# Hybrid decoder step on one core: the weight split of a mixture-of-experts loop, parts 4 and 5 moved across a branch

## The chip, the cores and the metric

The kernel runs on one core of a Trainium2 chip. The metric is device time in microseconds, the median of several runs. TensorE (PE) multiplies matrices, VectorE (DVE) and ScalarE (ACT) work element by element, GpSimd (POOL) issues gathers and scatters by index, and SyncE (SP) issues the loads. Each engine runs its own instructions in order and waits for others by semaphores.

## The reference

One layer of a decoder for 2048 prompt rows and 32 sample rows, 1024 wide: normalised input projection, dilated window attention beside a state-space mixer, output projection, and then a mixture of 32 experts, of which each row takes two. The change lies in the expert stage only:

```
def expert_block(args):
    xb, e = args
    hid = jax.nn.silu(xb @ w_gate[e]) * (xb @ w_up[e])
    return hid @ w_down[e]
# w_gate, w_up: (32, 1024, 512); w_down: (32, 512, 1024)
# y[token] = sum over its two experts of gate * expert_block(row)
```

All values are 32 bit floats. The kernel keeps their precision on PE by splitting each operand into a rounded part h and a rest l = x - h, and by adding three products, h*h, h*l and l*h.

## The kernel before

The routing stage leaves, for each expert in an order that it chooses (`R.order`), the number of its rows (`R.cnt`) and lists of row numbers in groups of 128. The function `moe` then runs 32 experts p = 0 to 31, unrolled, with instructions in the order of the text. One block (`block`) works on 128 rows of one expert. An expert with up to 128 rows runs only `main(p)`, one block. One with more runs one to three blocks of `further(p, b)` ahead of it, inside the branches at L2130, L2132 and L2134; the branch at L2130 is skipped for the small ones.

The weights of one expert come in six parts of 1 MB: parts 0 to 3 hold gate and up (two of eight slices of the 1024 rows each, 2 x 512 KB), parts 4 and 5 hold down. `E.load(p, i)` (L1906) issues part i of expert p on SP into the buffer `raw` i; there is one buffer for each part. `E.hi` (L1934) lets ACT cast the buffer to `wh`, `E.lo` (L1937) lets DVE subtract to get `wl`. A pair (wh, wl) lies in one of eight places; part i of expert p takes place (6p + i) mod 8, so that parts 2, 3, 4, 5 of the next expert take the places of parts 0, 1, 2, 3 of this one, and must wait until PE has read these. A load into a buffer waits for the subtraction that read it.

A block: PE multiplies slices 0 to 3 for both halves of the hidden width (`up`, L2003), then slices 4 to 7 for half 0, then it transposes the 128 x 1024 rows of the next block into PX (`turned`, L1993), then slices 4 to 6 of half 1; it transposes half 0 of the hidden values (`hidT(0)`, L2011), multiplies slice 7 of half 1, takes a quarter of the down product (L2020), transposes hidden half 1, and takes the other three quarters. Between these stand, on ACT and DVE, the Silu (L2006) and the product with up (L2007) for each half, the split hh, hl of the transposed hidden half (L133, L134), the split xh, xl of the next rows (`prepare`, with the same two lines), and on ACT the scaled output row of the block before (`store`, L2023), which POOL scatters.

The split of the weights hangs on four hooks of a block, `steps[0]` to `steps[3]`. `early(p)` is the first: parts 4 and 5 of this expert, the loads of parts 4 and 5 of the next, parts 0 and 1 of the next expert, and a load of part 0 for the one after. It runs in the first `further` block, or, where that is skipped, in `main` under a second branch (L2087). The other hooks of `main` split parts 2 and 3 of the next expert:

```
def early(p):
    convert(p, *LATE)                 # LATE = (4, 5)
    for i in LATE:
        E.load(p + 1, i)
    convert(p + 1, *EARLY)            # EARLY = (0, 1)
    if p + 1 < NE:
        E.load(p + 2, 0)
```

The order on each engine is the order of the text (a manual schedule). At a skipped branch each engine posts a semaphore update in place of the work that it skips.

Of the kernel before, what the change touches and what calls it, by code (L numbers as in the profile page):

```python
# [12 lines left out]
F32 = mybir.dt.float32  # L13
# [4 lines left out]
ALU = mybir.AluOpType  # L18
# [111 lines left out]
def split(K, h, l, src, hengine=None):  # L130

    nc = K.nc
    (hengine or nc.scalar.copy)(h, src)  # L133
    nc.vector.tensor_tensor(out=l, in0=src, in1=h.bitcast(F32), op=ALU.subtract)  # L134
# [1091 lines left out]
def ada_later(K, I, pool, small, psum, ready):  # L1226
# [4 lines left out]
    for chunks, cols in ((gate, (0, 512, 3072, 3584)), (ffn, (1024, 1536, 2048, 2560))):  # L1231

        def load(kt):
# [5 lines left out]
            return wt  # L1239

        wts = [load(0), load(1)]
        br = small()
        m = small()
# [622 lines left out]
def load_w(K, I, raw, e, i):  # L1866


    if isinstance(e, int):
        e = slice(e, e + 1)  # L1870
    if i < 4:
        for j, nm in enumerate(('gate', 'up')):
            src = I['w_expert_' + nm][0, e].rearrange("o (p k) f -> (o p) k f", k=8)[:, 2 * i:2 * i + 2]
            K.nc.sync.dma_start(out=raw[:, 1024 * j:1024 * j + 1024].rearrange("p (k f) -> p k f", k=2), in_=src)
    else:
        src = I['w_expert_down'][0, e, 256 * (i - 4):256 * (i - 4) + 256].rearrange("o (c p) n -> (o p) c n", p=128)
        K.nc.sync.dma_start(out=raw.rearrange("p (c n) -> p c n", c=2), in_=src)

LATE, EARLY = (4, 5), (0, 1)
BOTH, AT0, AT1 = 4, 7, 1


class Experts:
# [20 lines left out]
    def load(self, p, i):  # L1906

        if p >= 32:
            self.after(i)
            return  # L1910
        if not self.ready:
            self.later.append((p, i))
            return
        if i in (0, 1, 4):
            self.now = self.K.nc.sync.value_load(self.R.order[0:1, p:p + 1], min_val=0, max_val=31)
        load_w(self.K, self.I, self.RAW[i], bass.ds(self.now, 1), i)

# [24 lines left out]
def moe(K, I, E, first, h2_d, Y_d, R, TK, last):  # L1942
# [5 lines left out]
    V, G, A = nc.vector, nc.gpsimd, nc.scalar  # L1948
    NE = 32
    with ExitStack() as st:  # L1950
# [3 lines left out]
        PX = ps.tile([128, 8, 128], F32, name="px")  # L1954
# [4 lines left out]
        XH, XL = (w.tile([128, 8, 128], F32R, name=f"x{nm}") for nm in "hl")  # L1959
        X0, X1, Y = (w.tile([128, 1024], F32, name=nm) for nm in ("xg0", "xg1", "y"))  # L1960
# [6 lines left out]
        def convert(p, *parts):  # L1967

            for i in parts:
                if p < NE:  # L1970
                    E.hi(p, i)
                    E.lo(p, i)

        def gather(idx, x):
            nc.gpsimd.indirect_dma_start(out=x, out_offset=None, in_=h2_d,
                                         in_offset=bass.IndirectOffsetOnAxis(ap=idx, axis=0),
                                         bounds_check=2079, oob_is_err=False)

        def gather_first(p):
            if p < NE:  # L1980
                gather(R.src[:, p:p + 1], X0)

        def gather_second(p):
            if p < NE:
                more = nc.values_load(R.cnt[0:1, p:p + 1], engines=(mybir.EngineType.Pool,), min_val=0, max_val=2080)
                with tc.If(more > 128):
                    gather(R.src[:, 32 + p:33 + p], X1)

        def turned(x):

            for hf in range(2):
                for k in range(4):
                    nc.tensor.transpose(PT[hf][:, k, :], x[:, 4 * hf + k::8], K.ident)  # L1993

        def prepare():

            split(K, XH, XL, PX)

        def up(p, hf, ks):
            for k in ks:  # L2000
                wh, wl = E.up(p, k, hf)
                for j, (x, y) in enumerate(((XH, wh), (XH, wl), (XL, wh))):
                    nc.tensor.matmul(PU[hf], x[:, k, :], y, start=(k == 0 and j == 0), stop=(k == 7 and j == 2))  # L2003

        def act(hf):
            A.activation(HID[hf], PU[hf][:, 0:256], AF.Silu)  # L2006
            V.tensor_tensor(out=HID[hf], in0=HID[hf], in1=PU[hf][:, 256:512], op=ALU.mult)  # L2007

        def hidT(hf):
            for k in range(2):  # L2010
                nc.tensor.transpose(PT[2 + hf][:, k, :], HID[hf][:, 128 * k:128 * k + 128], K.ident)  # L2011
            split(K, HT[hf][0], HT[hf][1], PT[2 + hf][:, 0:2])
# [9 lines left out]
        def store(col):  # L2022
            A.activation(Y, PY, AF.Copy, scale=R.g[:, col:col + 1])  # L2023
            nc.gpsimd.indirect_dma_start(out=Y_d, out_offset=bass.IndirectOffsetOnAxis(ap=R.dst[:, col:col + 1], axis=0),  # L2024
                                         in_=Y, in_offset=None, bounds_check=2 * TK - 1, oob_is_err=False)

        def block(p, before, x, steps, label, hint):


            for k in range(BOTH):  # L2030
                up(p, 0, (k,))
                up(p, 1, (k,))
            steps[0]()
            if before is not None:
                store(before)
            steps[1]()
            up(p, 0, range(BOTH, 8))
            act(0)
            if x is not None:
                turned(x)  # L2040
            steps[2]()
            up(p, 1, range(BOTH, AT0))
            hidT(0)
            up(p, 1, range(AT0, 8))
            act(1)
            steps[3]()
            if label:
                tc.mark_branch_hint_location(label, hint=hint, engines=[mybir.EngineType.PE])
            for c in range(AT1):
                down(p, c)  # L2050
            hidT(1)
            if x is not None:
                prepare()
            for c in range(AT1, 4):
                down(p, c)

# [1 line left out]
            pass  # L2058

        def early(p):  # L2060
            convert(p, *LATE)
            for i in LATE:
                E.load(p + 1, i)
            convert(p + 1, *EARLY)
            if p + 1 < NE:
                E.load(p + 2, 0)

        def further(p, b):


            steps = [nothing] * 4
            if b == 0:
                steps[0] = lambda: early(p)
            else:
                steps[1] = lambda: gather(R.src[:, 32 * (b + 1) + p:32 * (b + 1) + p + 1], X1)
            before = 32 * (b - 1) + p if b else 96 + p - 1
            at = 128 * (b + 2)
            block(p, before if p or b else None, X1, steps, f"at{at}_{p}" if b < 2 else None, blocks[p] > at)

        def count(p):  # L2080
            if p < NE:
                blocks[p] = nc.values_load(R.cnt[0:1, p:p + 1], min_val=0, max_val=2080)

        def main(p):

            def begin():
                with tc.If(blocks[p] <= 128):  # L2087
                    early(p)

            more = p + 1 < NE  # L2090
            halves = slice(0, 1024), slice(1024, 2048)

            def second():
                gather_second(p + 1)
                if more:
                    E.load(p + 2, 1)
                    convert(p + 1, 2)
                    E.load(p + 2, 2)
                    E.hi(p + 1, 3, halves[0])

            def first():
                gather_first(p + 2)
                if more:
                    E.hi(p + 1, 3, halves[1])
                    E.lo(p + 1, 3, halves[0])

            def end():
                if more:
                    E.lo(p + 1, 3, halves[1])
                    E.load(p + 2, 3)  # L2110

            block(p, 64 + p, X0 if p + 1 < NE else None, (begin, second, first, end),
                  f"at128_{p + 1}" if p + 1 < NE else None, blocks[p + 1] > 128 if p + 1 < NE else None)

        gather(R.src0, X0)
# [1 line left out]
        for i in range(first, 4):  # L2117
            convert(0, i)
            E.load(1, i)
        gather_second(0)  # L2120
        turned(X0)
        prepare()
        gather_first(1)
        blocks = {}
        count(0)
        for p in range(NE):
            if p == NE - 1:
                last()
            count(p + 1)
            with tc.If(blocks[p] > 128, label=f"at128_{p}"):  # L2130
                further(p, 0)
                with tc.If(blocks[p] > 256, label=f"at256_{p}"):  # L2132
                    further(p, 1)
                    with tc.If(blocks[p] > 384, label=f"at384_{p}"):  # L2134
                        further(p, 2)
            main(p)
        store(96 + NE - 1)

# [16 lines left out]
        with tc.If(most > 512):  # L2155
# [9 lines left out]
            with tc.For_i(0, ns, 1) as it:  # L2165
# [29 lines left out]
                x, xt = X0, X1.rearrange("p (k t) -> p k t", k=8)  # L2195
# [233 lines left out]
```

## Time and profile before

| | us |
|---|---|
| median of 3 runs | 2709.98 |
| lowest and highest | 2707.05, 2711.68 |
| profiled execution | 2703.7 |
| its span | 2702.0 |
| PE busy | 2440.1 (90%) |
| DVE busy | 1423.7 (53%) |
| ACT busy | 1129.5 (42%) |
| POOL busy | 602.9 (22%) |

Busy time is an average over stages that have different limits, so the rows below are taken from the expert stage. Times are from the start of the span. Matmuls are pipelined: a matmul of 512 columns is shown with 0.39 us, and the next begins 0.23 us after it.

### The profile page before, as it was taken

Reading aid. Unit: us, or ns where it says so; the run is one execution under the profiler, and the core shown is the slowest. Engines: PE = TensorE matmul, PEld = TensorE weight load, DVE = VectorE, ACT = ScalarE, POOL = GpSimd, SP = SyncE. Lnnn points to the kernel's source line nnn. Section 1 sums busy time; section 2 is a strip of 40 time slices with the busy share of each in tenths; the row PEclk is TensorE's granted clock in tenths of the full one; section 3 lists DMA queues with packets and bytes.
Section 4 is the critical chain, followed back from the end, with each engine's and each line's share of the span. In section 5 each row is a group of like instructions: output and inputs, shape, how many; then the busy total and the mean of one; then the engine's idle time right before and its main releaser. Section 6 shows DMA issues by size and latency. Waiting matters only on the chain. (4 is left out here: it accounts for less than half of the span.)

```text
span 2702.0 us, 36257 instructions
## 1 busy us (share of the span) xinstructions
PE 2440.1 (90%) x12135; PEld 1897.1 (70%) x12135; DVE 1423.7 (53%) x2764; ACT 1129.5 (42%) x1625; POOL 602.9 (22%) x712
## 2 busy tenths in 40 slices
PE   6999899897879999997999949999999999999987
PEld 3766677664457789996777737787777777777763
DVE  4444311256053565663678664537456566667538
ACT  3222211133143444646444434536446556566522
POOL 1022100001001334443344411212122121222203
PEclk9999999798888998998999969999999999999998
DMA  7322311465753632113433335547557577878657
GB/s 277 85 107 99 108 59 51 151 230 184 221 159 112 197 92 62 36 31 113 131 125 117 123 140 219 214 150 291 183 213 281 198 263 267 298 285 304 240 211 297
DMA packets 239271, 467.68 MB, mean 173 GB/s; under 512 B 87764, under 2 KB 117636, under 8 KB 236943
## 3 DMA queue, kind: packets, MB, share of 16 engines
q1 hardware_dynamic: 211496, 411.95, 44.1%
q0 software_dynamic: 16304, 38.50, 3.9%
q10 hardware_dynamic: 11200, 13.83, 1.5%
q8 instruction: 144, 2.36, 0.3%
q14 instruction: 127, 1.04, 0.1%
HBM read 395.60 MB, written 88.44 MB: 179 GB/s over the span
## 5 line engine op out<-in xcount | busy, mean ns | idle before, releaser
L1939 DVE TENSOR_TENSOR wl<-raw,wh 128x2048 fp32r<-128x2048 f32 (+1 forms) x223 | 434.4, 1990 | 168.7 <-ACT wh L1935 168.1
L1935 ACT CAST wh<-raw 128x2048 fp32r<-128x2048 f32 (+1 forms) x223 | 359.9, 1667 | 95.4 <-PEq L2130 51.0
L2003 PE MATMUL pu<-wh,xh 128*128 128x512 f32 x816 | 333.9, 409 | 22.4 <-PEq L2130 15.5
L2003 PE MATMUL pu<-wh,xl 128*128 128x512 f32 x816 | 323.3, 396 | 0.8 <-issue 0.8
L2003 PE MATMUL pu<-wl,xh 128*128 128x512 f32 x816 | 322.8, 396 | 0.0
L2024 POOL DMA_INDIRECT Y_d<-y,Rdst x52 | 116.8, 2247 | 713.1 <-ACT y L2023 684.7
L206 PE MATMUL po<-wh,hh 128*128 128x512 f32 x512 | 209.0, 409 | 12.1 <-ACT hh L133 12.1
L206 PE MATMUL po<-wl,hh 128*128 128x512 f32 x512 | 206.6, 404 | 0.0
L206 PE MATMUL po<-wh,hl 128*128 128x512 f32 x512 | 203.0, 402 | 0.0
L2003 PEld LDWEIGHTS pu<-wh,xh 128*128 128x128 f32 x816 | 154.9, 190 | 65.8 <-issue 35.8
L2003 PEld LDWEIGHTS pu<-wh,xl 128*128 128x128 f32 x816 | 154.5, 189 | 35.8
L873 DVE CUSTOM_DVE_ANT_0 jk<-pa,mask 128x256 bf16<-128x256 f32 (+1 forms) x384 | 117.9, 362 | 112.8 <-PE pa L870 111.9
L2003 PEld LDWEIGHTS pu<-wl,xh 128*128 128x128 f32 x816 | 155.0, 190 | 30.3
L2020 PE MATMUL po<-wh,hh 128*128 128x512 f32 x408 | 169.6, 416 | 0.1
L2020 PE MATMUL po<-wh,hl 128*128 128x512 f32 x408 | 161.9, 397 | 0.0
L2020 PE MATMUL po<-wl,hh 128*128 128x512 f32 x408 | 161.3, 395 | 0.0
L939 PE MATMUL pb<-QS,KH 128*128 128x256 f32 (+1 forms) x384 | 150.3, 398 | 0.0
L216 ACT COPY ob<-po 128x512 f32<-128x512 f32 x64 | 37.6, 587 | 264.8 <-PE po L206 262.9
L942 ACT ACTIVATE PT<-pb 128x512 f32<-128x512 f32 (+1 forms) x152 | 89.9, 591 | 122.5 <-PE pb L940 120.6
L940 PE MATMUL pb<-QM,KL 65*128 65x256 f32 (+1 forms) x384 | 139.4, 370 | 1.3 <-DMA QM<-MR 1.3
L988 PE MATMUL pw<-PT,vb 128*128 128x128 f32 (+1 forms) x752 | 132.3, 312 | 0.0
L206 PEld LDWEIGHTS po<-wh,hh 128*128 128x128 f32 x512 | 99.1, 194 | 40.4 <-ACT hh L133 14.7
(588 smaller groups left out, 4913.7 us busy)
## 6 DMA issues: line engine op xcount, KB each, us to landing
raw<-w_expert_gate SPq DMA_DIRECT2D x128, 512.0 KB
raw<-w_expert_up SPq DMA_DIRECT2D x128, 512.0 KB
raw<-w_expert_down SPq DMA_DIRECT2D x64, 1024.0 KB
y<-Y_d SPq DMA_DIRECT2D x32, 512.0 KB
kr<-cache_k_win SPq DMA_DIRECT2D x56, 256.0 KB
kr<-cache_v_win SPq DMA_DIRECT2D x56, 256.0 KB
vb<-out_vp SPq DMA_DIRECT2D x96, 128.0 KB
wada<-w_ada_ffn SPq DMA_DIRECT2D x24, 512.0 KB
```

The source lines that it names most:

```text
L206: nc.tensor.matmul(out, a[:, kt, :], wt[c][:, kt], start=(kt == 0 and i == 0), stop=(kt == 7 and i == len(terms) - 1))
L216: nc.scalar.copy(ob, out)
L873: V.tensor_tensor_reduce(out=jk[:, o:o + n], in0=pt[:, o:o + n], in1=mask[:, 256 - n:256], op0=ALU.add, op1=ALU.max, scale=1.0, scalar=-3e ...
L939: nc.tensor.matmul(po, cols(KH, c0, step, 128), cols(QS, c0, step, nq), start=True, stop=False)
L940: nc.tensor.matmul(po, cols(KL, c0, step, 128), cols(QM, c0, step, nq), start=False, stop=True)
L942: A.activation(PT[:, :o], ps[:, :o], AF.Exp)
L988: nc.tensor.matmul(out, vt[h, b, idx], PT[:, o + q0:o + q0 + n_], start=start, stop=(final and Wd == W), skip_group_check=True)
L1935: self.K.nc.scalar.copy(self.part(p, i)[0][:, cs], self.RAW[i][:, cs])
L1939: self.K.nc.vector.tensor_tensor(out=wl[:, cs], in0=self.RAW[i][:, cs], in1=wh[:, cs].bitcast(F32), op=ALU.subtract)
L2003: nc.tensor.matmul(PU[hf], x[:, k, :], y, start=(k == 0 and j == 0), stop=(k == 7 and j == 2))
L2020: nc.tensor.matmul(PO[i], x[:, c % 2, :], y[:, cs], start=(c == 0 and j == 0), stop=(c == 3 and j == 2))
L2024: nc.gpsimd.indirect_dma_start(out=Y_d, out_offset=bass.IndirectOffsetOnAxis(ap=R.dst[:, col:col + 1], axis=0), in_=Y, in_offset=None, bou ...
```

## The change

Part 4 of the next expert is cast and subtracted, and part 5 cast, in the last block of the expert before, ahead of the branch at L2130: the first half of part 4 is cast ahead of the split of hidden half 0, the rest behind the split of hidden half 1. Part 5 is subtracted in `early`, behind the branch. `prepare` becomes two functions: ACT's cast of the next rows goes ahead of the quarter of the down product, DVE's subtraction stays. Part 3 is cast in one piece. The load of part 4 goes behind the branches, ahead of `main(p)`; for the first expert, its part 4 and the cast of its part 5 go ahead of the loop.

```
-LATE, EARLY = (4, 5), (0, 1)
+LATE, EARLY = 5, (0, 1)
...
-        if i in (0, 1, 4):
+        if i in (0, 1, 4, 5):
             self.now = self.K.nc.sync.value_load(self.R.order[0:1, p:p + 1], min_val=0, max_val=31)
...
         def prepare():
-            split(K, XH, XL, PX)
+            A.copy(XH, PX)
+
+        def prepare2():
+            V.tensor_tensor(out=XL, in0=PX, in1=XH.bitcast(F32), op=ALU.subtract)
...
             up(p, 1, range(BOTH, AT0))
+            steps[3]()
             hidT(0)
             up(p, 1, range(AT0, 8))
             act(1)
-            steps[3]()
+            steps[4]()
+            if x is not None:
+                prepare()
             if label:
                 tc.mark_branch_hint_location(label, hint=hint, engines=[mybir.EngineType.PE])
             for c in range(AT1):
                 down(p, c)
             hidT(1)
             if x is not None:
-                prepare()
+                prepare2()
+            steps[5]()
...
         def early(p):
-            convert(p, *LATE)
-            for i in LATE:
-                E.load(p + 1, i)
+            E.lo(p, LATE)
+            E.load(p + 1, LATE)
             convert(p + 1, *EARLY)
...
-                    E.hi(p + 1, 3, halves[0])
+                    E.hi(p + 1, 3)
...
-                    E.hi(p + 1, 3, halves[1])
                     E.lo(p + 1, 3, halves[0])
 
-            def end():
+            def mid():
+                if more:
+                    E.hi(p + 1, 4, halves[0])
+
+            def third():
                 if more:
                     E.lo(p + 1, 3, halves[1])
                     E.load(p + 2, 3)
 
-            block(p, 64 + p, X0 if p + 1 < NE else None, (begin, second, first, end),
+            def end():
+                if more:
+                    E.hi(p + 1, 4, halves[1])
+                    E.lo(p + 1, 4)
+                    E.hi(p + 1, LATE)
+
+            block(p, 64 + p, X0 if p + 1 < NE else None, (begin, second, first, mid, third, end),
...
+        convert(0, 4)
+        E.load(1, 4)
+        E.hi(0, LATE)
         gather_second(0)
         turned(X0)
         prepare()
+        prepare2()
...
+            if 0 < p:
+                E.load(p + 1, 4)
             main(p)
```

## Rows read from the trace of the kernel before

**Rows 1.** Windows: stretch, length, busy PE, PEld, DVE, ACT, POOL, clock, DMA share, GB/s.
```profile
1624.40:2613.80 989.40, 939.46 (x4273) 744.98 (x4274) 564.61 (x476) 524.51 (x527) 194.15 (x100) 0.99 0.66 240
```

**Rows 2.** Waits of PE and of its weight loads in that stage: total, times, longest.
```profile
PE pt L2011 <- DVE hid L2007: 32.8, 19, 2.0
PE pu L2003 <- PEq L2130: 15.5, 20, 6.2
...
PEld pt L2011 <- DVE hid L2007: 40.9, 19, 2.4
```

**Rows 3.** The branch L2130 by engine: durations in ns, minimum/median/maximum.
```profile
L2130 PEldq COMPARE_BRANCH  x32: 77/372/6687, 1617.4 to 2575.5; - x32
...
L2130 DVEq EVENT_SEMAPHORE  x20: 21/21/21, 1621.9 to 2519.8; - x20
```

**Rows 4.** Windows of the transposes L2011 alone: three experts, then the stage.
```profile
1720.00:1740.60 20.60, 0.82 (x4) 0.48 (x4) 1.00 0.71 265
1740.60:1760.70 20.10, 0.82 (x4) 0.48 (x4) 1.00 0.92 342
1760.70:1833.90 73.20, 3.04 (x16) 2.23 (x16) 1.00 0.40 145
...
1624.40:2613.80 989.40, 40.12 (x204) 27.16 (x204) 0.99 0.66 240
```

**Rows 5.** Timeline of PE, two blocks: start, length, and idle time before it.
```profile
1701.40 0.39 PE L2003 MATMUL pu<-wh,xh 128*128 128x512 f32 x1
...
1711.76 0.39 PE L2003 MATMUL pu<-wh,xl 128*128 128x512 f32 x1
...
1712.68 0.38 PE L2011 MATMUL pt<-ident,hid 128*128 128x128 f32 x2
...
1719.99 0.47 PE L2003 MATMUL pu<-wh,xh 128*128 128x512 f32 x1 [0.30 <-PEq L2130]
...
1733.29 0.44 PE L2011 MATMUL pt<-ident,hid 128*128 128x128 f32 x2 [1.91 <-DVE hid L2007]
...
1740.67 0.47 PE L2003 MATMUL pu<-wh,xh 128*128 128x512 f32 x1 [0.30 <-PEq L2130]
```

**Rows 6.** Timeline of DVE, the same two blocks.
```profile
1715.97 0.42 DVE L134 TENSOR_TENSOR hl<-pt,hh 128x256 fp32r<-128x256 f32 x1 [0.20 <-ACT hh L133]
1716.89 1.23 DVE L134 TENSOR_TENSOR xl<-px,xh 128x1024 fp32r<-128x1024 f32 x1 [0.49 <-ACTq L2130]
1721.80 11.10 DVE L1939 TENSOR_TENSOR wl<-raw,wh 128x2048 fp32r<-128x2048 f32 x5 [3.69 <-ACT wh L1935]
1732.82 0.41 DVE L2007 TENSOR_TENSOR hid<-hid,pu 128x256 f32<-128x256 f32 x1
```

**Rows 7.** Timeline of ACT, the same two blocks.
```profile
1710.17 1.04 ACT L1935 CAST wh<-raw 128x1024 fp32r<-128x1024 f32 x1
1713.16 0.37 ACT L133 CAST hh<-pt 128x256 fp32r<-128x256 f32 x1 [1.95 <-PE pt L2011]
...
1715.57 0.37 ACT L133 CAST hh<-pt 128x256 fp32r<-128x256 f32 x1 [1.38 <-PE pt L2011]
...
1719.86 7.34 ACT L1935 CAST wh<-raw 128x2048 fp32r<-128x2048 f32 x4 [3.01 <-PEq L2130]
1727.11 1.11 ACT L2023 ACTIVATE y<-po,Rg 128x1024 f32<-128x1024 f32 x1
```

**Rows 8.** The loads: SP's issues of parts 4 and 5, sizes, windows of transfers.
```profile
1724.12 2.58 SPq L1877 DMA_DIRECT2D raw<-w_expert_down  x2
...
raw<-w_expert_down SPq DMA_DIRECT2D x62, 1024.0 KB
...
1746.00:1764.00 18.00, 16.04 (x76) 12.72 (x75) 16.53 (x13) 14.66 (x15) 6.16 (x3) 1.00 1.01 373
```

**Rows 9.** PE after one skip, and the windows of its clock behind it.
```profile
1955.93 0.77 PE L2003 MATMUL pu<-wh,xh 128*128 128x512 f32 x1 [3.69 <-PEq L2130]
...
1956.00:1961.00 5.00, 5.00 (x12) 3.94 (x13) 3.27 (x2) 5.00 (x3) 0.00 (x0) 0.50 0.17 66
```

More of the change, by code (lines that the diff above doesn't have):

```diff
@@ L2068, in further @@
         def further(p, b):
-            steps = [nothing] * 4
+            steps = [nothing] * 6
             if b == 0:
```

## The prediction

> **What bounds the kernel now.** I read the windows first. The expert stage runs from 1624.4 to 2613.8 us, 989 us of a span of 2702; there TensorE (PE) is busy for 939 us, VectorE (DVE) for 565 and ScalarE (ACT) for 525 [rows 1]. PE is the bound, and only a change of its idle time counts. The waits of PE say where that is: 19 times the transposes of the hidden half (L2011) wait for DVE's product (L2007), 32.8 us in all on the matmul's side, 40.9 on the weight load's, 2.0 to 2.4 at most each. All else the profile lists there is branches [rows 2]. The branch at L2130 runs 32 times and is skipped 20 times [rows 3]: 20 experts of up to 128 rows run one block ("single"), 12 run the rest. The transposes, four to a block, are 204 in the stage, so 51 blocks; counted by stretch they give the order: single, single, four blocks of a longer expert, single, single, ... [rows 4]; the same count over the rest never gives more than two singles in a row.
>
> PE's rows show the price. From first matmul to first matmul, a last block before a skip takes 1719.99 - 1701.40 = 18.6 us and the single that follows 1740.67 - 1719.99 = 20.7. In the first the transposes start 11.28 us after the block, in the second 13.30 [rows 5]. So a stall costs 2.0 us, 19 x 2.0 = 38 us in all, inside the 32.8 and 40.9 above. (The twentieth single ran, after an idle PE, in a stretch with a granted clock of 0.50, 1.2 GHz, in which PE was late itself [rows 9].)
>
> Why is DVE late? In the single it runs five subtractions of 2.2 us from 1721.80 on (parts 4, 5 of this expert, 0, 1, 2 of the next), and only then the product, at 1732.82, 12.8 us into the block [rows 6]. ACT has four casts (7.34 us), the output row (1.1) and one and a half casts more before its Silu, and it sat idle for 3.0 us before them, until PE had passed the branch [rows 7].
>
> **The change part by part.** *Front of a single.* Three casts (5.5 us of ACT) and one subtraction (2.2 us of DVE) leave it; the cast of part 3 comes whole ahead of the Silu (+0.9). DVE: part 5 needs no cast any more, so it starts some 0.2 us into the block, and four times 2.2 end at 9.0. ACT: two casts at 1.83 (7.34 / 4), the row 1.1, casts 2 and 3 again 3.7, ends at 8.6 (9.3 if it starts 0.9 late), Silu 0.4. Product done by 9.4 to 10.0, wanted at 11.28: at least 1.2 us to spare, so the stall goes whole: -38. What is late next is the matmul queue itself.
>
> *End of a main block, DVE.* After the second hl (1715.97) come xl (1.23 alone) and now part 4's subtraction (11.10 / 5 = 2.22): 1715.97 + 0.42 + 1.23 + 2.22 = 1719.84, or 1719.76 with the overlap of 0.1 that such rows show [rows 6], against the next block's first matmul at 1719.99 [rows 5]. This matters at the 20 skips: a skipped branch makes each engine finish its own work and then post a counter [rows 3], and the first matmul waits for DVE's and ACT's counters. DVE's post now comes 0.15 to 0.2 us before PE wants it, where xl ends at 1718.12 today. Price: below by 0; above by 1 us at each of the 20 skips = 20 if the row slips. I take 0.1 each, 2 us. Beyond a skip PE falls through on direct waits, and part 4 is not read for 12 us: nothing.
>
> *End of a main block, ACT.* hh (1715.57, 0.37), half a part 1.04, part 5 1.83 [rows 7]: ends 1718.8, over 1 us before the next block. Hidden.
>
> *Half of part 4 in the middle.* It waits for the last matmul that reads the old part 2 (start 1711.76, end 1712.15 [rows 5]), takes 1.04 and ends at 1713.2; the hh cast starts at 1713.16 today [rows 7]. In-order ACT may hold hh, and with it the down products, by 0 to 0.1 us in 31 blocks: 0 to 3 us, taken 1. ACT is idle there, so no other loss.
>
> *XH earlier.* ACT is idle for 1.38 us before the second hh [rows 7]; the cast has half a part's shape, 1.04. Nothing, in all 51 blocks; if the room were gone, 51 x the overhang. The subtraction xl keeps its place in DVE's order.
>
> *SP, DMA, POOL.* Each main block but the first has part 4's load (one issue of 1 MB) moved past the branch, and part 5 reads the expert's number again: SP only. Today SP issues the loads of 4 and 5 at 1724.12, 4.1 us into the single [rows 8], behind the subtractions; afterwards part 4 goes at about 1 us, part 5 at 2.6, and the queue behind them up to 4 us earlier. Part 4 must now land by the middle (11 us) instead of the next block's start. POOL's scatter starts about 2 us earlier. Ahead of the loop, two casts, one subtraction and a load are added beside PE's 6.2 us wait on the first branch [rows 2]: hidden, at most 2.3 us once without that cover.
>
> Sum: -38 + 2 + 1 = -35. Made against the profiled 2703.7 us: 2669. That execution is 6.3 us below the median of the timed runs, 2709.98; I forecast the median, 2675.
>
> **Rules weighed.** Transfers move 373 GB/s with the DMA engines fully busy (share 1.01) for 18 us [rows 8]. The Trainium skill (DMA: Bandwidth & Descriptors, Where 436 GB/s comes from) puts the bound for HBM to SBUF at about 358 GB/s per core; the trace is above that. By the page a single, with 7.3 MB, could not be shorter than 20.5 us, nearly its length today, and the change would be worth almost nothing, 2709.
>
> PE's branch takes 0.08 to 6.7 us [rows 3], and once PE stood 3.7 us at a skip [rows 9]. The Trainium skill (Runtime: NRT & Kernel Launch, Instruction fetch mechanics) says that a taken branch out of the instruction window stalls for a fetch; PE's rows agree. For ACT and DVE, which now come to the skip without idle time, no row shows what it would cost. At an estimate of 1 us for each of 20 skips the sum would be -15 by the page; by the rows it stays -35.
>
> **Rivals.**
> 1. *The end of the block becomes the bound* (DVE's post late by 0.5 to 1.2 us at 20 skips, or ACT and DVE pay 1 us at the jump that idle time hid). For: the margin is 0.2 us. Against: the terms are constant from block to block. Gain 38 - 10 to 24 = 14 to 28, about 2690.
> 2. *Transfers bound the singles.* Six parts of 1.05 MB, one scatter and one gather of 0.5 are 7.3 MB; at 373 GB/s 19.7 us against the 18.6 that PE wants. With no store of loaded parts each of 19 singles gains 1.0: 19 us, 2691. Against: at most two singles come together, and the loads of a pair up to the last needed part (8.4 MB) take 23 us, ending some 6 us into the second, where it is wanted at 11.
> 3. *ACT or DVE is held at the skip until SP's counters*, so that the front starts 3 us late as now: product at 12.5, the stall back at 1.2 to 2 us. Nearly no change, 2700 to 2710. Against: SP's loads now end earlier.
> 4. *Slower: part 4 lands too late for the middle.* ACT is in order, so the cast that waits holds hh and the second Silu, and PE stands. It decides from 11 us into the block, 10 us after the issue; alone the 1 MB takes 2.8 us, behind four others 14. Then 3 us at 20 singles and as much again in the longer experts' last blocks where the queue is full, up to 31 x 3 = 93 against 38. With half of that, 2720. Against: two parts at most are queued ahead of it.
>
> **How the numbers follow.** Forecast 0.70 (own range 2662 to 2686: 0 to 6 us of the small terms, and the jitter of 2707 to 2712 that the runs before show); rival 1 0.11, rival 2 0.06, rival 3 0.07, rival 4 0.06. From these the range is 2660 to 2698: it leaves out rivals 3 and 4 and some of the tails. A measurement here can tell about 0.2%, 5.4 us: faster has the forecast, rivals 1 and 2, 0.87; same 0.07; slower 0.06.
>
> **What would show it.** Right: the 19 waits of L2011 for L2007 go from PE's list; the product comes 9 to 10 us after the first matmul of a single; singles take 18.2 to 18.8 us; DVE runs to within 0.3 us of a skip. Wrong: PE's waits at the branch (15.5 us in all now [rows 2]) grow by over 4 us (rival 1), DVE's or ACT's first part waits for a transfer (2, 3), or the down products wait for hh for over 0.5 us (4). The forecast falls if a median over 2698 comes with the L2011 waits gone.

## The result and the profile after

The changed kernel takes 2664.15 us (median of 4 runs, 2659.85 to 2666.08) beside 2708.52 for the kernel before (4 runs, 2698.14 to 2711.68): ratio 0.984, 95% interval 0.981 to 0.987. Taken again on another occasion it was 2666.15 beside 2706.27, ratio 0.984 [0.982, 0.986]. So it is faster, by 44 us in the first comparison and by 40 in the second, and 2664 lies within the range forecast, near its lower end. The profiled execution took 2664.0 us (span 2662.3), so profile against profile the gain is 39.7 us.

The expert stage, from the first matmul to the same place behind the last block, as [rows 1] (stretch, length, busy PE, PEld, DVE, ACT, POOL, clock, DMA share, GB/s):

```profile
1625.00:2574.20 949.20, 932.04 (x4274) 745.32 (x4275) 558.70 (x475) 524.07 (x525) 167.60 (x100) 0.99 0.69 250
```

The stage is 40.2 us shorter with the same work on it. PE's idle time went from 989.4 - 939.5 = 49.9 us to 949.2 - 932.0 = 17.2, which is 32.8 less: as much as the old wait in [rows 2]. The other 7.4 us left PE's busy time. Some 3 of them are how the records overlap (matmuls shown with 0.39 us start 0.23 apart, so each of 19 gaps looked 0.16 shorter than it was); 2.5 are time at the lower clock in blocks 11 and 17, below; the rest is open.

PE's waits in the stage, as [rows 2] (line waited for, total, times, longest):

```profile
PE pu L2006 <- PEq L2149: 9.9, 5, 5.9
PE pu L2006 <- DVEq L2149: 4.8, 15, 0.4
PE pu L2006 <- PEq L2151: 3.9, 7, 0.6
...
PEld pt L2014 <- DVE hid L2010: 0.3, 1, 0.3
```

(Lines have moved: `up` is L2006, the transposes L2014, the product L2010, the branch L2149.) The 19 waits for the product are gone; one weight load, in the first block, keeps 0.3 us. The waits at the branch are 9.9 + 4.8 = 14.7 us at 20 skips against 15.5 before: they did not grow, though at 15 of them DVE's post is now named as the last to come.

PE around the same single as [rows 5] (start, length, idle time before and what ended it):

```profile
1719.04 0.47 PE L2006 MATMUL pu<-wh,xh 128*128 128x512 f32 x1 [0.30 <-PEq L2149]
...
1730.26 0.38 PE L2014 MATMUL pt<-ident,hid 128*128 128x128 f32 x2
...
1737.54 0.47 PE L2006 MATMUL pu<-wh,xh 128*128 128x512 f32 x1 [0.30 <-DVEq L2149]
```

The single takes 18.5 us where it took 20.7, and its transposes come 11.22 us after its start, with nothing waited for. DVE and ACT in it, as [rows 6, 7]:

```profile
1715.36 1.21 DVE L2000 TENSOR_TENSOR xl<-px,xh 128x1024 fp32r<-128x1024 f32 x1
1716.49 2.28 DVE L1939 TENSOR_TENSOR wl<-raw,wh 128x2048 fp32r<-128x2048 f32 x1
1719.27 8.90 DVE L1939 TENSOR_TENSOR wl<-raw,wh 128x2048 fp32r<-128x2048 f32 x4 [0.49 <-PEq L2149]
1728.08 0.41 DVE L2010 TENSOR_TENSOR hid<-hid,pu 128x256 f32<-128x256 f32 x1
```

```profile
1714.88 2.86 ACT L1935 CAST wh<-raw 128x1024 fp32r<-128x1024 f32 x2
1718.98 3.72 ACT L1935 CAST wh<-raw 128x2048 fp32r<-128x2048 f32 x2 [1.24 <-PEq L2149]
...
1727.50 0.38 ACT L2009 ACTIVATE hid<-pu 128x256 f32<-128x256 f32 x1 [0.18 <-PE pu L2006]
1729.77 1.05 ACT L1935 CAST wh<-raw 128x1024 fp32r<-128x1024 f32 x1 [1.89 <-PE pu L2006]
```

Part 4's subtraction ends at 1718.77, 0.27 us ahead of PE's first matmul; behind the skip DVE starts 0.23 us after that matmul, ends four subtractions and has the product at 9.04 us into the block. It is done at 9.45, 1.8 us before it is wanted. The half cast of part 4 at 1729.77 waits for PE, not for its load, which SP issued 11 us sooner:

```profile
1718.80 3.16 SPq L1877 DMA_DIRECT2D raw<-w_expert_down  x2
```

Block by block (counted from 0), from first weight load to first weight load: 15 of the 19 stalled blocks lost 1.9 to 2.2 us each (30.8 in all), the first block 1.5, block 11 3.6, block 16 2.7 and block 12 nothing, 38.6 together. In block 12 a pause of PE's weight loads between two matmuls, for which the profile names no cause, grew from 1.02 to 2.26 us and took the place of 1.36 us of stall. Block 16 ends in the long pause at a branch of [rows 9], which was 0.7 us shorter (2.95 instead of 3.69), so only 2.0 of its 2.7 are the stall. Three blocks without a stall gave 2.0 more: 0.9 in block 17, where the stretch at the lower clock behind that pause was shorter, 0.7 in block 25, where another pause without a named cause was shorter, and 0.3 in block 19. Block 11 lost more than its stall because of the clock. Windows of the kernel before, over the end of block 11 and over the one after the skip that [rows 9] show:

```profile
1834.00:1847.00 13.00, 11.53 (x53) 9.24 (x53) 11.19 (x6) 12.15 (x9) 4.22 (x2) 1.00 0.59 226
1847.00:1856.00 9.00, 8.64 (x31) 6.36 (x31) 4.92 (x7) 2.04 (x4) 0.81 (x1) 0.81 1.00 383
...
1955.90:1963.00 7.10, 7.07 (x20) 5.64 (x21) 5.27 (x3) 7.10 (x4) 0.00 (x0) 0.61 0.38 125
```

Block 11's stall (1.77 us on the matmul's side) lies across the border of the first two rows, and in the second the granted clock is 0.81, a mixture of full (2.4 GHz) and half (1.2 GHz): the rest of that block took 1.6 us longer. Of the other stalls none left such a row in this execution. So the stalls alone were worth about 36 us here, and the clock and PE's unexplained pauses make up the rest.

### The profile page after: what moved, and what is told of

Same layout as the page of the kernel before. It is cut to its first block, busy times and chain, and to the rows that moved or that the text cites. A ratio compares the mean times of both kernels' runs of the same rounds, so it can differ in the third digit from the quotient of the medians.

```text
span 2662.3 us, 36279 instructions
## 1 busy us (share of the span) xinstructions
PE 2433.9 (91%) x12135; PEld 1898.9 (71%) x12135; DVE 1419.9 (53%) x2764; ACT 1132.3 (43%) x1625; POOL 574.8 (22%) x712
## 3 DMA queue, kind: packets, MB, share of 16 engines
q14 instruction: 125, 1.02, 0.1%
## 5 line engine op out<-in xcount | busy, mean ns | idle before, releaser
L2006 PE MATMUL pu<-wh,xh 128*128 128x512 f32 x816 | 333.6, 409 | 21.0 <-PEq L2149 9.9
L2006 PE MATMUL pu<-wh,xl 128*128 128x512 f32 x816 | 323.1, 396 | 2.1 <-issue 2.1
L2006 PE MATMUL pu<-wl,xh 128*128 128x512 f32 x816 | 323.1, 396 | 0.0
L2027 POOL DMA_INDIRECT Y_d<-y,Rdst x52 | 91.9, 1768 | 679.6 <-ACT y L2026 647.7
L2006 PEld LDWEIGHTS pu<-wh,xh 128*128 128x128 f32 x816 | 154.8, 190 | 65.6 <-issue 32.3
L2006 PEld LDWEIGHTS pu<-wh,xl 128*128 128x128 f32 x816 | 154.5, 189 | 35.6
L2006 PEld LDWEIGHTS pu<-wl,xh 128*128 128x128 f32 x816 | 154.8, 190 | 30.0
```

## Experiments

Each is an edit of the changed kernel, but for the third, an edit of the one before. Ratios are to the kernel before on the same chip.

**Part 4 subtracted behind the branch** (e1). Casts of 4 and 5 stay at the end of the block.

```diff
         def early(p):
+            E.lo(p, 4)
+            E.load(p + 1, 4)
             E.lo(p, LATE)
...
                     E.hi(p + 1, 4, halves[1])
-                    E.lo(p + 1, 4)
                     E.hi(p + 1, LATE)
...
-            if 0 < p:
-                E.load(p + 1, 4)
             main(p)
```

> The changed kernel, but DVE's subtraction of part 4 stays behind the branch, in the front of the block (both casts stay ahead of it), and the load of part 4 follows it there. Theory D (in a single the product waits for DVE's queue of subtractions): five subtractions of 2.2 us from 0.2 us into the block and 0.4 for the product end at 11.6 to 11.7 us, wanted at 11.2; a stall of 0.4 to 0.5 us comes back in 19 to 20 singles, 8 to 10 us over the changed kernel: about 2673 us, some 35 below before. Theory A (it waits for ACT's casts, which start only behind the branch): ACT's front is that of the changed kernel, so no stall comes back: 2664 us, less up to 2 us because nothing of DVE's stands before the skip.

Measured: 2668.95 us (2663.17 to 2669.26), 0.985 [0.984, 0.987]. PE's waits, and DVE in the single:

```profile
PE pu L2006 <- PEq L2149: 7.7, 19, 2.4
```

```profile
1716.03 11.10 DVE L1939 TENSOR_TENSOR wl<-raw,wh 128x2048 fp32r<-128x2048 f32 x5 [2.33 <-PEq L2149]
1727.05 0.41 DVE L2010 TENSOR_TENSOR hid<-hid,pu 128x256 f32<-128x256 f32 x1
```

DVE again has five subtractions in front of the product, as before the change, yet the stall of 2 us is not back. What is left of it shows on the weight loads' side alone:

```profile
PEld pt L2014 <- DVE hid L2010: 4.9, 18, 0.4
```

That is 0.3 us a single. What differs from [rows 6] is only when DVE starts. There it waited until ACT had cast part 4, 1.81 us into the single (1721.80 - 1719.99); here it starts with the single. At the end of the block DVE's post is early again, and the DVEq row is gone, with no gain from that. The time came out between the two expectations, 5 us over the change, which is about what can be told apart at all.

**Part 5 cast behind the branch** (e2).

```diff
         def early(p):
-            E.lo(p, LATE)
+            convert(p, LATE)
...
                     E.lo(p + 1, 4)
-                    E.hi(p + 1, LATE)
...
```

> The changed kernel, but ACT's cast of part 5 stays behind the branch, in the front of the block. Theory D: the first subtraction waits for that cast, so four of 2.2 us start 2.0 us into the block and the product ends at 11.2 to 11.3 us, wanted at 11.2: a stall of 0 to 0.3 us in 19 singles, 0 to 6 us over the changed kernel (2664 to 2670 us). Theory A: three casts at 1.83, the output row 1.1, two casts more, Silu 0.4 and the product 0.4 end at 11.1: also 0 to 3 us. A third theory, that all three moved pieces are needed (each worth a third of the gain), expects about 13 us more, 2677.

Measured: 2672.49 us (2669.20 to 2677.70), 0.987 [0.985, 0.989], 8 us over the change, but none of it in the steady singles, which keep 18.6 and 17.9 us and no wait. The wait that came back is one, in the very first block:

```profile
PE pt L2014 <- DVE hid L2010: 3.1, 1, 3.1
```

```profile
1627.28 1.28 ACT L1935 ACT_TABLE_LOAD   x1 [5.42 <-SPq L2147]
1628.58 5.51 ACT L1935 CAST wh<-raw 128x2048 fp32r<-128x2048 f32 x3
1634.11 1.28 ACT L2026 ACT_TABLE_LOAD   x1
```

Only there does ACT load three tables of 1.28 us (the third before the Silu) around its casts, so a third cast ahead of the Silu shows: that block is 3.2 us longer than with the change. Block 12 is 2.6 us longer: its pause without a named cause was 3.2 us, and the granted clock fell behind it, as it did in e1, e3 and e8 at pauses of 2.6 to 2.9 there.

The steady singles show something else. DVE's first subtraction behind the branch waits for a cast again, now part 5's, and starts 1.89 us into the single (first matmul at 1723.45), as late as before the change:

```profile
1725.34 8.90 DVE L1939 TENSOR_TENSOR wl<-raw,wh 128x2048 fp32r<-128x2048 f32 x4 [2.15 <-ACT wh L1935]
1734.15 0.41 DVE L2010 TENSOR_TENSOR hid<-hid,pu 128x256 f32<-128x256 f32 x1
```

But only four subtractions follow, and the product starts 10.70 us in, in time. So a late start alone does not make the stall either; it takes the late start and five subtractions.

**The rows' split and part 3's cast alone** (e3, on the kernel before).

```diff
         def prepare():
-            split(K, XH, XL, PX)
+            A.copy(XH, PX)
+        def prepare2():
+            V.tensor_tensor(out=XL, in0=PX, in1=XH.bitcast(F32), op=ALU.subtract)
...
-                    E.hi(p + 1, 3, halves[0])
+                    E.hi(p + 1, 3)
...
```

> The kernel before with only the order of the rows changed: the cast of the next rows (XH) goes ahead of the branch hint and of the first quarter of the down product, and part 3 is cast in one piece; parts 4 and 5 stay where they were. Theory D and theory A: DVE still has five subtractions ahead of the product in a single, the 19 stalls stay, within 3 us of before. Rival: the earlier XH shortens the end of every block (51 of them), 0.1 to 0.2 us each: 5 to 10 us below before.

Measured: 2710.31 us, 1.000 [0.999, 1.001], and the old wait stands:

```profile
PE pt L2014 <- DVE hid L2010: 34.1, 19, 3.6
```

So these two parts of the change cost and give nothing by themselves, within 3 us. In this execution three of the singles with a stall (blocks 5, 26 and 42) were some 1.5 us longer than in the one before: their down products took 7.0 to 7.2 us instead of 5.6, as in block 11 there.

**Half a subtraction more at the end** (e4): DVE's post comes 1.2 us later.

```diff
                     E.hi(p + 1, 4, halves[1])
+                    E.lo(p + 1, 4, halves[0])
                     E.lo(p + 1, 4)
```

> The changed kernel with half a part's subtraction (1.14 us of DVE) done twice, at the end of a main block ahead of the branch. Theory of the margin: a skipped branch lets DVE post its counter only when its own work is done, and the next block's first matmul waits for it; with 0.0 to 0.2 us of margin each of the 20 skips becomes 0.9 to 1.1 us longer: 18 to 22 us over the changed kernel, 2682 to 2686. Rival: PE needs nothing of DVE at the block's start; the product comes 1.1 us later with over 1 us to spare, so 0 to 3 us.

Measured: 2687.94 us (2683.98 to 2689.76), 0.992 [0.991, 0.993], 24 us over the change:

```profile
PE pu L2006 <- DVEq L2150: 35.0, 19, 5.8
```

The pause of PE's weight loads went from 0.70 to 0.82 us to 1.97 to 2.08 at 18 of the 20 skips (not at the first and not behind block 16): 1.3 us for 1.2 us of work. So there is no room left at the end of the block: the subtraction put there by the change ends at about the point from which more would cost.

**Part 4's load far behind** (e5): ahead of part 3's cast, behind the load of part 2 for the expert after next. (SP's register then holds the number of another expert when part 3 is issued, so part 3's values are another expert's; sizes and count of the loads are the same.)

```diff
                     E.load(p + 2, 2)
+                    if 0 < p:
+                        E.load(p + 1, 4)
                     E.hi(p + 1, 3)
...
-            if 0 < p:
+            if p == NE - 1:
                 E.load(p + 1, 4)
             main(p)
```

> The changed kernel with the load of part 4 issued in the middle of a main block, behind the loads of parts 5, 0, 1 and 2, in place of its start. Theory (the middle decides: ACT is in order, so a cast that waits for its load holds the split of the hidden half and the second Silu): in a single the load goes out at about 9.5 us behind 4 MB and lands at 16 to 19 us, the cast wants it at 11, so PE stands 5 to 8 us in each of 20 singles and 2 to 4 in 11 longer experts' last blocks: 120 to 190 us over the changed kernel, slower than before (2785 to 2855). Rival: the loaded parts have enough lead that the time of one issue does not matter: 0 to 5 us.

Measured: 2989.97 us, 1.105 [1.101, 1.108], 324 us over the repeat of the change, about twice as much lost as expected.

```profile
PE po L2023 <- ACT hh L133: 264.4, 30, 11.6
```

```profile
1746.20 1.04 ACT L1935 CAST wh<-raw 128x1024 fp32r<-128x1024 f32 x1 [12.65 <-DMA raw<-w_expert_down]
1747.15 0.37 ACT L133 CAST hh<-pt 128x256 fp32r<-128x256 f32 x1
```

```profile
1740.00:1746.00 6.00, 0.00 (x0) 0.00 (x0) 0.00 (x0) 0.00 (x0) 0.00 (x0) 0.59 0.91 367
1746.00:1752.00 6.00, 4.43 (x13) 3.51 (x14) 2.46 (x5) 3.49 (x6) 0.00 (x0) 0.56 0.26 74
```

The chain is rival 4's: ACT waits for the transfer, the split hh stands behind it in ACT's order, the down products behind hh. In the single shown (first matmul at 1724.72) the load went out at 10.7 us, not 9.5, and its data came at 21.5, not at 16 to 19. It hits 30 blocks, the longer experts' last ones too (4.2 to 6.2 us each, the singles 9.7 to 11.6). 264 us are waits. The down products that follow run partly at the lower clock (0.56 in the second row) and take 6.9 to 8.5 us from the first to the last of the 24, instead of 5.6: 61 us in 30 blocks. Together that is 326, against 321 between the two spans; the pauses of PE behind block 16 and inside block 12, some 6 us with the clock behind them, are gone here.

**Part 4's load somewhat behind** (e9): the same, ahead of the load of part 1.

```diff
                 if more:
+                    if 0 < p:
+                        E.load(p + 1, 4)
                     E.load(p + 2, 1)
                     convert(p + 1, 2)
...
```

> The load of part 4 is issued in the block itself, ahead of the load of part 1 for the expert after next, so about 5 us later in a single than with the whole change and some 6 us sooner than in the kernel that had it behind the load of part 2 (2990). Its data are wanted at 10.5 to 11 us into the block. Theory (rival 4's mechanism, decided by the order on SP's queue): issued at 5 to 6 us with up to two parts of 2.8 us ahead of it, it lands at 11 to 14 us; the half cast in the middle of a single waits 1 to 3 us and PE stands for as long: 20 x 1 to 3 = 20 to 60 us over the change, 2685 to 2725, the longer experts unharmed since SP runs ahead there. Rival (two parts fit ahead of the middle, the queue is empty enough): no wait in the middle, 2662 to 2670.

Measured: 2777.16 us (2775.03 to 2780.38), 1.026 [1.024, 1.028].

```profile
PE po L2023 <- ACT hh L133: 82.7, 19, 5.7
```

```profile
1730.49 1.04 ACT L1935 CAST wh<-raw 128x1024 fp32r<-128x1024 f32 x1 [5.49 <-DMA raw<-w_expert_down]
```

```profile
1718.70:1730.50 11.80, 9.76 (x48) 7.83 (x47) 8.07 (x5) 6.15 (x6) 4.77 (x2) 1.00 0.85 313
...
1732.00:1736.00 4.00, 4.00 (x13) 3.06 (x14) 2.86 (x5) 2.54 (x5) 0.00 (x0) 0.61 1.02 412
```

The direction is the theory's, the size is not: 4.4 us of wait in 19 of the 20 singles instead of 1 to 3. The issue came 6.7 us into the single (first matmul at 1716.16), and part 4 was there 7.6 us later: since 1718.7, when part 5 was issued, 313 GB/s x 11.8 us = 3.7 MB had moved. That fits parts 5, 0 and 4 in the order of their issue, with 0.5 MB of POOL's, and leaves next to nothing for parts 1 and 2, issued behind part 4. The longer experts stayed whole, as expected. The second share of the loss is the clock: behind 17 of the 19 waits the down products took 7.0 to 8.5 us instead of 5.6 (in the row shown at a granted clock of 0.61 over 4 us), 35 us in all; behind the other two (3.3 and 3.5 us) the clock stayed at 1.00. 82.7 and 35 are 118, against 111 us between the spans; the pauses behind block 16 and inside block 12 are gone here too.

**Part 4 in halves at the end** (e6): its first half is subtracted one step earlier, and part 3 whole ahead of that, so DVE's post comes 1.2 us sooner.

```diff
                 if more:
-                    E.lo(p + 1, 3, halves[0])
+                    E.lo(p + 1, 3)
+                    E.load(p + 2, 3)
...
             def third():
                 if more:
-                    E.lo(p + 1, 3, halves[1])
-                    E.load(p + 2, 3)
+                    E.lo(p + 1, 4, halves[0])
...
                     E.hi(p + 1, 4, halves[1])
-                    E.lo(p + 1, 4)
+                    E.lo(p + 1, 4, halves[1])
```

> The changed kernel with DVE's work at the end of a main block spread: part 3 is subtracted whole ahead of the split of hidden half 0 (and its load issued there), half of part 4 in the place that this leaves, the other half behind xl. DVE's end comes 1.1 us earlier. Theory of the margin: the 15 waits of PE for DVE's counter at skips (4.8 us in all) are gone, and what stays is PE's own drain of 0.3 us there: 0 to 2 us below the changed kernel. Rival: the whole subtraction of part 3 (2.2 us) holds the split of hidden half 0, and each of 31 blocks gets 0.2 to 0.5 us longer: 6 to 15 us over it.

Measured: 2669.19 us (2664.93 to 2670.21), 0.985 [0.982, 0.987], no gain over the change:

```profile
PE pu L2006 <- PEq L2149: 17.6, 20, 6.6
```

All 20 skips go back to PE's own branch, and the steady singles keep 18.50 and 17.93 us. With e4 this says that DVE's post was level with PE's own end and cost next to nothing.

**The branch hint 4 us earlier** (e7).

```diff
             act(0)
+            if label:
+                tc.mark_branch_hint_location(label, hint=hint, engines=[mybir.EngineType.PE])
             if x is not None:
                 turned(x)
...
-            if label:
-                tc.mark_branch_hint_location(label, hint=hint, engines=[mybir.EngineType.PE])
             for c in range(AT1):
```

> The changed kernel with PE's branch hint placed behind the first Silu, some 4 us earlier in each block. Theory: the gaps that PE shows at some skips and fall-throughs (3.3 us at one skip, with a stretch at a granted clock of 0.5 behind it) are instructions of the target that come late; a hint 4 us earlier takes 3 to 6 us off: 2658 to 2661. Rival: the hint is used up by the branches in between, or the gaps come from the transfers of weights beside the fetch: no change, within 2 us, or a longer branch at all 32, up to 10 us over.

Measured: 2664.16 us (2661.09 to 2666.18), 0.984 [0.981, 0.986], the same as the change. The one long skip (behind block 16, 3.3 us on the weight loads' side with the change) was still 3.2 us. A hint 4 us earlier does not shorten it. It is not fixed, though: in e5 and e9, where PE had stood for 10 and 5 us in block 16 itself, it is 0.7 us like any other skip. That fits something that comes at its own time and that PE's wait covers; what it is, no run shows.

**Only part 4's cast moved** (e8). The subtraction, the load and all of part 5 go back behind the branch.

```diff
         def early(p):
-            E.lo(p, LATE)
+            E.lo(p, 4)
+            E.load(p + 1, 4)
+            convert(p, LATE)
             E.load(p + 1, LATE)
...
                     E.hi(p + 1, 4, halves[1])
-                    E.lo(p + 1, 4)
-                    E.hi(p + 1, LATE)
...
```

> Of the change, the weights' share at the end of a main block is cut to one thing: the two half casts of part 4. Part 4's subtraction and its load, and part 5 whole, go back behind the branch. Theory A (what the stall of 2.0 us came from is the cast that DVE had to wait for at the front of a single, 1.8 us, and not the amount of work there): DVE starts its five subtractions within 0.4 us of a single's first matmul, ends them at about 11.5 us, the product at 11.9 against 11.3 wanted less what PE's queue hides; singles 18.5 to 18.9, as with part 5's cast early and the subtraction behind: 2664 to 2672, product wait 0 to 0.5 us each. Rival B (all moved pieces count, each for its share of 5.5 us of casts and 2.2 of subtraction): two casts of 1.83 and a subtraction of 2.2 back in the front bring 1 us or more of stall to 19 singles, 2683 to 2695.

Measured: 2670.89 us (2664.39 to 2673.65), 0.986 [0.984, 0.988]: theory A. Part 4's cast, moved, brings 37 of the 40 to 44 us, on top of the rows' split and part 3's cast, which alone bring nothing (e3). ACT and DVE in the single that starts at 1723.43:

```profile
1723.31 5.54 ACT L1935 CAST wh<-raw 128x2048 fp32r<-128x2048 f32 x3 [2.97 <-PEq L2147]
```

```profile
1723.32 11.10 DVE L1939 TENSOR_TENSOR wl<-raw,wh 128x2048 fp32r<-128x2048 f32 x5 [2.35 <-PEq L2147]
1734.34 0.41 DVE L2010 TENSOR_TENSOR hid<-hid,pu 128x256 f32<-128x256 f32 x1
```

```profile
PE pu L2006 <- PEq L2147: 14.8, 20, 6.1
...
PE pt L2014 <- DVE hid L2010: 2.0, 1, 2.0
```

ACT has three casts in front, DVE five subtractions, nearly all that stood there before; but they start together, and the product comes at 10.9 us. The one wait of 2.0 us is the first block's. What the five subtractions still cost is again some 0.3 us a single, as in e1.

**The changed kernel again**: the repeat named with the result.

> The changed kernel once more beside the three below, on the same chip: 2664 us, 0.982 to 0.987 of before.

Measured: 2666.15 us (2662.13 to 2668.28), 0.984 [0.982, 0.986], with the same waits at the skips:

```profile
PE pu L2006 <- DVEq L2149: 4.6, 14, 0.4
```

## Why the prediction was right, step by step

- *The stall goes whole, -38.* Right in the mechanism: the wait row is gone, and the blocks that had it lost 38.6 us. The closeness of the two numbers is partly luck: 1.6 of the 38.6 are the clock in block 11 and 0.7 a shorter pause behind block 16, while block 12 gave nothing, which leaves about 36 for the stalls. The reason given, that three casts and one subtraction leave the front, was more than needed. Before, DVE's late start, its five subtractions and the product added up: 1.81 + 11.0 + 0.4 = 13.2 us, against 11.3 wanted, which is the stall of 2.0. Taking away the late start is enough (e1, e8, five subtractions still there); taking away one subtraction is enough too (e2, the start still 1.89 us late). The change did both, and so had 1.8 us to spare. e1, e2 and e8 have part 4's cast ahead of the branch in common; e3, without it, keeps the stall. The forecast of the product, done by 9.4 to 10.0 us, was right: 9.45.
- *DVE at the end of the block, +2.* The place was right, the price was next to 0: the subtraction ends 0.27 us ahead of PE's matmul, and at 18 of the 20 skips the weight loads' pause is 0.70 to 0.82 us, where it was 0.69 to 0.95 before. That this was a brink e4 shows, +1.3 us a skip for 1.2 us more, and e6, nothing gained for 1.2 us less.
- *The half cast in the middle, +1.* Cost nothing: the weight loads that wait for hh sum to 12.9 us in 51 blocks, at most 0.3 each, and to 13.2 before.
- *Other edits at nothing.* e3 agrees for the rows and part 3. Ahead of the loop the stage starts at 1625.0 instead of 1624.4, which tells nothing, as the kernels here start it anywhere from 1622.0 to 1630.8; e2 shows that a cast there is worth something to the first block.
- *The forecast of 2675.* 11 us too high. 4.7 of them are the sum: -35 against -39.7, that is the two terms of +2 and +1 that cost nothing, and 2 us more that no step named (the clock in blocks 11 and 17, shorter pauses of PE behind block 16 and in block 25, less what block 12 did not give). The other 6.3 are the step from the profiled time to the median: the execution before lay 6.3 us under its median, the one after at its median (2664.02 and 2664.15). That the offset would be kept was assumed, and no row spoke for it.
- *Rival 1* (end of the block): not here, 14.7 us at the branch against 15.5; e4's 1.2 us more, which cost 1.3, show that no margin was left. The other half of the rival, a jump that costs DVE or ACT 1 us, is an assumed price that no row gave. DVE's branch instruction itself takes (duration in ns, minimum/median/maximum; before, then after):

```profile
L2130 DVEq COMPARE_BRANCH  x32: 43/56/72, 1621.3 to 2575.9; - x32
L2149 DVEq COMPARE_BRANCH  x32: 43/56/67, 1623.5 to 2536.2; - x32
```

  DVE's whole pause at a skip with the change, post and waits included, is 0.49 us at 18 of the 20. (The 0.49 in [rows 6] is another thing: xl waiting for ACT's xh.) The Trainium skill (Runtime: NRT & Kernel Launch, Instruction fetch mechanics) would have it that a taken branch out of the window stalls for a fetch; for DVE at these 18 skips the trace shows no stall of that size, and the estimate of -15 that hung on it falls. Whether it is what PE's pause behind block 16 is made of, no run shows.
- *Rival 2* (transfers): no part was late in the singles: ACT's first cast behind a skip starts after the same 1.24 us of idle time at all of them but the first, and its later casts wait for PE or for nothing. It came close: over the window of a single in the changed kernel the DMA engines are nearly full (a window of 19 us, then the single's own),

```profile
1738.00:1757.00 19.00, 19.00 (x90) 15.37 (x89) 16.92 (x13) 16.03 (x15) 5.92 (x3) 1.00 0.97 368
1737.50:1755.40 17.90, 17.86 (x83) 14.53 (x84) 15.54 (x12) 14.92 (x14) 5.92 (x3) 1.00 0.97 365
```

  The single there takes 17.9 us, and at 365 GB/s 6.5 MB moved in it, not the 7.3 of the prediction, so its estimate of 19.7 us was too high too. The Trainium skill (DMA: Bandwidth & Descriptors, Where 436 GB/s comes from) has about 358 GB/s as the bound from HBM to SBUF; the trace is above it, with 368 over 19 us here and 412 over 4 us in e9. The estimate of 20.5 us that hung on the page's figure falls with it.
- *Rival 3* (ACT or DVE held for SP): no. ACT's first cast behind the skip waits 1.24 us, named for PE's or DVE's post (at four skips for a load, with the same length), DVE 0.49; SP's post is the last only at the first block.
- *Rival 4* (part 4 too late): not here, the load goes 0.2 us ahead of the block and is wanted 10.7 us in. The mechanism is real: e9, issued at 6.7 us, loses 113 us over the change, e5 324. Both its steps were told rightly, the price was not: 4.4 us at 19 blocks and on average 1.8 more for the clock in e9, where 3 us at 20 was written.

## What to carry to other kernels

Where one engine waits at the front of a block for another's first result, add up its late start and its work against the time at which its own result is wanted, and move the smallest piece that brings the sum under it: here one cast of 1.8 us, moved across a branch, was worth nearly all that moving a cast more and a subtraction was. Before putting work ahead of a branch that all engines pass, find which engine posts last and how far ahead of the bound engine: here work up to that point was free, and 1.2 us beyond it cost 1.3 at nearly every skip. A load that moves needs the queue counted at its new place: in e9 the two parts ahead of it were paid for in full.

## What the runs showed of the hardware that was not expected

- A wait of PE can cost more than its length, when the granted clock falls. On the matmul's side: in the kernel before, 18 of the 19 stalls (0.9 to 2.0 us) left the down products behind them at 5.6 us, and one (1.77 us) left 0.81 over the 9 us of its row, 1.6 us lost; in e3 three singles lost as much behind such stalls. Behind 17 of the 19 waits of 3.3 to 5.7 us in e9, and behind all 30 of 4.2 to 11.6 us in e5, the down products took 6.9 to 8.5 us instead of 5.6, 2 us more on average.
- One core's loads reached 408 to 412 GB/s over 4 us with the DMA engines full (e9), above the 373 of [rows 8].
- PE pauses at places for which the profile names no other engine: on the weight loads' side 2.8 to 4.1 us at the branch behind block 16 in ten of the twelve profiled executions, and 0.6 to 3.2 us between two matmuls inside block 12. Only e5 and e9, where PE waits for long in blocks 16 and 11, ahead of these places, show neither. In the first comparison alone such pauses changed single blocks by up to 1.2 us, and the runs of the changed kernel spread over 6 us, so a difference of 5 us between two kernels is not yet an effect.
